# Layer 1 of a two-layer trunk: split weights kept in DRAM for the second half, the layer norm's channel adds on GpSimd with its mean products a step later

## The chip, the cores and the metric

The kernel runs on one core of a Trainium2 chip. The metric is the device time of one execution in microseconds (us). Each kernel is executed several times; the median counts, and one further execution is recorded by the hardware profiler, which gives the traces shown here. Line numbers (L1208) are those of the kernel before.

## The reference, cut to what matters

Layer 0 (attention and a gated MLP) is not touched. The change lies in layer 1, a causal convolution module over 2048 rows (tokens) of 1024 channels:

```python
def conv_layer(h, w_in, dw_w, dw_b, ln_g, ln_b, w_out):
    a, gl, z = jnp.split(h @ w_in, 3, axis=-1)        # h: (1, 2048, 1024), w_in: (1024, 3072)
    y = a * jax.nn.sigmoid(gl)
    y = lax.conv_general_dilated(y, dw_w[:, None, :], ...,  # depthwise, causal, 31 taps
                                 feature_group_count=CONV_WIDTH) + dw_b
    y = jax.nn.silu(layer_norm(y, ln_g, ln_b))        # norm over the 1024 channels
    return (y * jax.nn.silu(z)) @ w_out
...
x = x + rms_norm(conv_layer(rms_norm(x, g_pre), ...), g_post)
```

All of it is float32.

## The kernel before, in words

A float32 product is made of three: each operand is split into a rounded high part and a low part (`split`: a cast on ScalarE, ACT, and a subtraction, L125, on GpSimd, POOL, or VectorE, DVE), and high x high, high x low and low x high are summed in PSUM. 

Layer 1 (`tail`, from about 1520 us on) handles the rows in two halves of 1024. For each half, `layer1_in` runs 12 blocks, eight gated inputs ("g": a and gl for 128 channels) and four z gates ("z": 256 channels); the strings in `GATED` give their order in half 0 and half 1. Each block has one weight of 1024 x 256, four groups of 24 matmuls on TensorE (PE), and a `yield` behind each group, called a step here. `weights` keeps one weight ahead: at the start of a block the next one is loaded from the input into the one buffer `wraw`, and split into `whi` and `wlo`, of which there are two pairs, A and B, used in turn. All 12 weights are loaded and split in each half, so twice in all.

A gated input goes to a buffer `y` (six of them, also used as scratch by the norm) and into a queue of convolutions. A convolution is 31 taps on 128 channels x 1024 rows. DVE does a tap by one multiply-add into PSUM (`acc`, L1135); POOL does one by an add (L1102) of a product from ACT (L1101). A planner shares the taps out as the program is written: `beat` moves a clock on by 5.12 us a step, and emits taps for an engine while the engine's own clock, kept by `busy` with written costs (a POOL add 2.4, a weight split 4.5, a DVE tap 1.2 or 1.33), is behind. `drain` emits all that is left of some convolutions. Results go to DRAM (`yc_d`), as the z gates do (`z_d`). All DMAs are issued by SyncE (SP), in order.

The layer norm works on chunks of 256 rows with channels on the partitions (`gated_norm`, a generator of eight steps): load eight channel blocks from `yc_d`; add the blocks up (L1215 for 1024 columns, `fold` L1203 and L1204 for 512 and 256) and let PE sum over the partitions with a matrix of 1/1024 (`mean`, L1208); subtract, square (ACT), add (L1225, POOL); fold again, a second product for the variance; square root and reciprocal; load z and scale (L1246); silu on ACT and the product with z on POOL (L1254); split for the next product. The adds of L1215, L1203 and L1204 are on DVE, and the product is emitted in the same step as they are. In `tail`, `l(c, m)` runs chunk c's norm up to step m. Chunks 0 to 2 have most of their steps inside half 1; chunks 3 to 7 run one per output chunk.

The output projection (`out2`) takes a chunk as two tiles of 128 rows with two groups of 24 matmuls each; DVE and POOL then do the rms norm, the residual add (L875) and SP the store. Its weight comes in four pieces (`wout_pieces`), each loaded raw (pieces 0, 1 and 2 through `wraw`, piece 3 through `h6`), cast on ACT and subtracted on DVE, while half 1 ends.

The program is laid out by a scheduler when it is built: it places instructions on their engines roughly in the order written, but lets one pass another that is not ready in its own reckoning. On the chip each engine runs its list in order.

Of the kernel before, what the change touches and what calls it, by code (L numbers as in the profile page):

```python
# [19 lines left out]
P = 128  # L20
# [24 lines left out]
GATED = "ggggzggzggzz", "gggggzggzgzz"  # L45
# [36 lines left out]
class Trunk:  # L82
# [151 lines left out]
    def setup(self):  # L234
# [15 lines left out]
        self.z_d = dr.tile([D, S], F32, name="z_d", tag="z_d")  # L250
        self.taps = self.tile(c, [P, KT, TAPS], F32, "taps")
# [554 lines left out]
    def wout_pieces(self, W, raws, places, which, w, lo):  # L806

        nc = self.nc
        w = w if w else {}
        for i in which:  # L810
            n, h = divmod(i, 2)
            w[n, h] = [self.tile(pool, [P, 4, 512], F32R, *tag) for pool, *tag in places[i]]
            pool, tag, *bufs = raws[i]
            raw = self.tile(pool, [P, 4, 512], F32, tag, *bufs)
            nc.sync.dma_start(raw, W[512 * h:512 * h + 512, 512 * n:512 * n + 512]
                              .rearrange("(k p) n -> p k n", p=P))
            self.split(*w[n, h], raw, nc.scalar, lo)
        return w
# [139 lines left out]
    def layer1_in(self, inner, half, hs):  # L958
# [5 lines left out]
        def load():  # L964
# [3 lines left out]
            kind, k = self.plan[i]  # L968
            if kind == "g":
# [9 lines left out]
            where, tag = ((pool, "A"), (inner, "B"))[i % 2]  # L979
            hi = self.tile(where, [P, KT, 256], F32R, "whi" + tag)  # L980
            lo = self.tile(where, [P, KT, 256], F32R, "wlo" + tag)
            self.split(hi, lo, raw, nc.scalar, nc.gpsimd)
            self.busy("p", 4.5)
# [192 lines left out]
    def gated_norm(self, c, hand):  # L1176
# [25 lines left out]
        def fold(s):  # L1202
            v.tensor_tensor(s[:, 0:2], s[:, 0:2], s[:, 2:4], ALU.add)  # L1203
            v.tensor_tensor(s[:, 0], s[:, 0], s[:, 1], ALU.add)  # L1204
# [10 lines left out]
        v.tensor_tensor(s, Y[0], Y[1], ALU.add)  # L1215
        fold(s)
        m = mean(s)
        self.busy("v", 2.1)
        yield
# [9 lines left out]
        fold(sq[0])  # L1229
        var = mean(sq[0])  # L1230
        self.busy("v", 0.9)
        yield
# [38 lines left out]
    def tail(self, w1):  # L1271

        with ExitStack() as ctx:
# [44 lines left out]
            for i in range(1, 44):  # L1318
                step(z)
                for c in range(3):  # L1320
                    l(c, min(7, i + 1 - c))
# [3 lines left out]
            wout = lambda which, w=None: self.wout_pieces(self.a["odd_w_out"][0], [(lp, "wraw")] * 3 + [(lp, "h6")], places, which, w, self.nc.vector)  # L1325
# [6 lines left out]
            w = wout([2, 3], w)  # L1332
            for c in range(n):
# [9 lines left out]
                step((t0, t0)[c == 0]), self.beat(5.12 if c == 0 else 0)  # L1343
# [68 lines left out]
```

## Time and profile before

| | us |
|---|---|
| runs (three) | 2270.82 to 2274.74 |
| median | 2273.02 |
| the profiled execution | 2272.01 |
| its span (first to last instruction) | 2270.3 |

| engine | busy us | share of the span |
|---|---|---|
| PE (matmul) | 2201.3 | 97% |
| DVE | 1548.2 | 68% |
| ACT | 1258.6 | 55% |
| POOL | 1400.1 | 62% |

The mean granted clock of PE over the span is 0.993 of the full one. In the views below, a wait "PE A L1208 <- DVE y L1204" says that PE stood idle before an instruction of line 1208, and that what ended last before it could start was DVE's instruction of line 1204. A wait for several things is put down to the last of them, so a name can mislead where that engine had long been done. A group's "x16" is its number of instructions. A stretch "1860.00:1865.00" is in us from the start of the span.

### The profile page before, as it was taken

The numbers are of one execution on the slowest core, as the hardware profiler recorded it, in microseconds if no ns is written. First come the engines' busy times: TensorE is split into PE (matmuls) and PEld (weight loads), VectorE is DVE, ScalarE is ACT, GpSimd is POOL, SyncE is SP. The second block draws the span as 40 slices with busy tenths as digits, with TensorE's granted clock in tenths as the row PEclk, the third lists the DMA queues.
The fourth block names the chain that finished last, engine by engine and source line by source line (L and its number), as shares of the span: only waits on it lengthen the run. The fifth ranks groups of instructions, "written<-read, shape, count | busy, mean of one in ns | idle before, by whom it ended". The sixth has DMA issues, their size and how long they took to land.

```text
span 2270.3 us, 34584 instructions
## 1 busy us (share of the span) xinstructions
PE 2201.3 (97%) x12414; PEld 1905.8 (84%) x12414; DVE 1548.2 (68%) x3273; ACT 1258.6 (55%) x2345; POOL 1400.1 (62%) x1350
## 2 busy tenths in 40 slices
PE   8999999999989999999999999999999989998998
PEld 7898889988878999898998978888888778886877
DVE  3441324465248998888889954518998899999772
ACT  5231232253258888878888863435555475556463
POOL 5231222243237778667779644548998579999683
PEclk9999999999989999999999999999999999999999
DMA  6352231442281111100113154651222432224641
GB/s 157 98 195 84 79 107 53 148 136 85 89 234 52 35 41 29 29 20 27 29 55 109 44 176 152 225 174 47 84 85 81 140 104 65 75 93 151 220 167 65
DMA packets 244860, 229.19 MB, mean 101 GB/s; under 512 B 33841, under 2 KB 206897, under 8 KB 244432
## 3 DMA queue, kind: packets, MB, share of 16 engines
q1 hardware_dynamic: 244688, 226.98, 31.6%
q8 instruction: 98, 1.61, 0.3%
q14 instruction: 74, 0.61, 0.1%
HBM read 157.73 MB, written 69.21 MB: 100 GB/s over the span
## 4 chain that ended last, share of the span: by engine, by line
PE 64%; DVE 14%; POOL 10%; issue 5%; ACT 3%; DMA 2%; SPq 1%; DVEq 0%; POOLq 0%; ACTq 0%
POOL cacc L1102 8%; PE T L708 7%; PE A L161 7%; PE A L162 7%; PE A L163 7%; DVE acc L1135 6%; PE O L731 4%; PE A L576 4%; PE O L730 4%; PE A L577 4%; PE A L842 4%; PE A L843 4%; PE A L844 4%; PE A L173 2%; PE A L175 2%
## 5 line engine op out<-in xcount | busy, mean ns | idle before, releaser
L1135 DVE SCALAR_TENSOR_TENSOR acc<-y,const_taps,acc 128x1024 f32<-128x1024 f32 x304 | 378.9, 1282 | 4.0
L1102 POOL TENSOR_TENSOR cacc<-cacc,prod 128x1024 f32<-128x1024 f32 x145 | 371.7, 2570 | 14.6 <-ACT prod L1101 7.4
L125 POOL TENSOR_TENSOR wlo<-wraw,whi 128x2048 fp32r<-128x2048 f32 (+1 forms) x26 | 120.9, 4649 | 314.2 <-ACT whi L122 279.3
L125 DVE TENSOR_TENSOR ptl<-T,pth 128x512 fp32r<-128x512 f32 (+1 forms) x414 | 263.8, 659 | 20.8 <-ACT pth L122 18.0
L122 ACT CAST pth<-T 128x512 fp32r<-128x512 f32 (+1 forms) x414 | 221.9, 580 | 51.4 <-PE T L708 41.1
L1101 ACT ACTIVATE prod<-y,const_taps 128x1024 f32<-128x1024 f32 x145 | 165.2, 1149 | 140.8 <-POOL cacc L1102 140.6
L161 PE MATMUL A<-hhi,whi 128*128 128x512 f32 x608 | 237.8, 391 | 0.0
L163 PE MATMUL A<-hhi,wlo 128*128 128x512 f32 x608 | 236.7, 389 | 0.0
L162 PE MATMUL A<-hlo,whi 128*128 128x512 f32 x608 | 236.7, 389 | 0.0
L685 POOL TENSOR_SCALAR Ps<-Ps,attn_ssm,gates 128x256 f32<-128x256 f32 (+15 forms) x128 | 161.9, 1265 | 112.1 <-DVE attn_ssm L682 78.2
L730 PE MATMUL O<-pth,V 128*128 128x256 f32 x824 | 220.5, 292 | 0.0
L731 PE MATMUL O<-ptl,V 128*128 128x256 f32 x824 | 219.4, 293 | 1.1 <-POOL ptl L717 0.4
L576 PE MATMUL A<-K,q 128*128 128x320 f32 (+4 forms) x544 | 206.8, 384 | 9.1 <-DVE attn_smx L580 4.4
L577 PE MATMUL A<-K,q 128*128 128x320 f32 (+4 forms) x544 | 183.6, 343 | 0.0
L680 ACT ACTIVATE Ps<-Ps,attn_nm 128x256 f32<-128x256 f32 (+15 forms) x128 | 155.9, 1218 | 31.4 <-DVE attn_nm L678 29.3
L580 DVE CUSTOM_DVE_ANT_1 Ps<-A,attn_bm 128x512 f32<-128x512 f32 (+3 forms) x264 | 154.8, 611 | 22.8 <-PE A L577 11.4
L708 PE MATMUL T<-ident,Ps 128*128 128x128 f32 x1088 | 164.2, 273 | 2.2 <-DVE ptl L125 1.8
L731 PEld LDWEIGHTS O<-ptl,V 128*128 128x128 f32 x824 | 155.4, 189 | 8.6 <-DVE ptl L125 4.2
L730 PEld LDWEIGHTS O<-pth,V 128*128 128x128 f32 x824 | 155.6, 189 | 2.5
L161 PE MATMUL A<-h,whiB 128*128 128x512 f32 x384 | 149.7, 390 | 1.2 <-ACT b L1026 1.2
L162 PE MATMUL A<-h,whiA 128*128 128x512 f32 x384 | 150.8, 393 | 0.0
L161 PE MATMUL A<-h,whiA 128*128 128x512 f32 x384 | 149.8, 392 | 0.7 <-DVE y L1008 0.7
(388 smaller groups left out, 6198.1 us busy)
## 6 DMA issues: line engine op xcount, KB each, us to landing
wraw<-in_even_w_in_dram SPq DMA_DIRECT2D x24, 1024.0 KB, 6.0
q<-q_d SPq DMA_DIRECT2D x128, 128.0 KB, 2.8
wraw<-in_odd_w_in_dram SPq DMA_DIRECT2D x32, 512.0 KB, 4.6
x<-x_d SPq DMA_DIRECT2D x21, 512.0 KB, 3.4
a_d<-osum SPq DMA_DIRECT2D x128, 64.0 KB, 2.1
x<-in_x_dram SPq DMA_DIRECT2D x16, 512.0 KB, 5.5
x_d<-x SPq DMA_DIRECT2D x16, 512.0 KB, 2.9
wraw<-in_odd_w_in_dram SPq DMA_DIRECT2D x8, 1024.0 KB, 5.0
```

The costliest lines, as they stand in the source:

```text
L122: self.nc.scalar.copy(hi, src)
L125: lo_eng.tensor_tensor(lo, src, hi.bitcast(F32), ALU.subtract)
L161: nc.tensor.matmul(o, whi[:, k, wk], hhi[:, k], start=(k == 0), stop=False)
L162: nc.tensor.matmul(o, whi[:, k, wk], hlo[:, k], start=False, stop=False)
L163: nc.tensor.matmul(o, wlo[:, k, wk], hhi[:, k], start=False, stop=(k == KT - 1))
L576: nc.tensor.matmul(out, q[:, 0, r, :], K[:, g, ks], start=True, stop=False)
L577: nc.tensor.matmul(out, q[:, 1, r, :], K[:, g, ks], start=False, stop=True)
L708: nc.tensor.transpose(pt[:, c:c + P], ps[r], self.ident)
L730: nc.tensor.matmul(O, v, hi[:, c], start=(i + j == 0), stop=False)
L731: nc.tensor.matmul(O, v, lo[:, c], start=False, stop=(i + j == len(items) - 1))
L1102: nc.gpsimd.tensor_tensor(c["sum"], c["sum"], t, ALU.add)
L1135: v.scalar_tensor_tensor(acc, win, w, old, ALU.mult, ALU.add)
```

## The change

Half 0 stores every split weight (high and low part, 1 MB each) in a new DRAM buffer `w_d`, and half 1 loads both parts from there straight into `whi` and `wlo`; the planner counts no split for them. In half 1 the order of blocks has the last gated input two blocks earlier. In the layer norm the adds of the channel blocks go from DVE to POOL, with new written costs, and each mean product is emitted a step after its adds. The norms of chunks 0 to 2 start two steps later and lie three steps apart instead of one. Chunk 1's norm is finished ahead of the first output group, and one norm step in each output chunk lies earlier than before. Output weight pieces 1 and 3 are loaded and split in two parts each, through the small buffers `b4`; pieces 0 and 2 use `wraw`.

```diff
--- before.py
+++ after.py
@@ -42,7 +42,7 @@
 LEFT, RIGHT = 96, 224
 LATE = 2
 OUT1 = [5, 7, 6, 4, 1, 3, 2, 0, *range(8, NT)]
-GATED = "ggggzggzggzz", "gggggzggzgzz"
+GATED = "ggggzggzggzz", "ggggggzggzzz"
 LEAD = 5.12
 AHEAD = 8.0
 
@@ -248,6 +248,7 @@
         self.x1_d = dr.tile([S, D], F32, name="x1_d", tag="x1_d")
         self.yc_d = dr.tile([D, S], F32, name="yc_d", tag="yc_d")
         self.z_d = dr.tile([D, S], F32, name="z_d", tag="z_d")
+        self.w_d = dr.tile([12, 2, P, KT * 256], F32, name="w_d", tag="w_d")
         self.taps = self.tile(c, [P, KT, TAPS], F32, "taps")
         self.cb = self.tile(c, [P, KT], F32, "cb")
         self.ident = self.tile(c, [P, P], F32, "ident")
@@ -811,10 +812,12 @@
             n, h = divmod(i, 2)
             w[n, h] = [self.tile(pool, [P, 4, 512], F32R, *tag) for pool, *tag in places[i]]
             pool, tag, *bufs = raws[i]
-            raw = self.tile(pool, [P, 4, 512], F32, tag, *bufs)
-            nc.sync.dma_start(raw, W[512 * h:512 * h + 512, 512 * n:512 * n + 512]
-                              .rearrange("(k p) n -> p k n", p=P))
-            self.split(*w[n, h], raw, nc.scalar, lo)
+            r = 2 if bufs else 4
+            for k in range(0, 4, r):
+                raw = self.tile(pool, [P, r, 512], F32, tag, *bufs)
+                nc.sync.dma_start(raw, W[512 * h + P * k:512 * h + P * (k + r), 512 * n:512 * n + 512]
+                                  .rearrange("(k p) n -> p k n", p=P))
+                self.split(*(t[:, k:k + r] for t in w[n, h]), raw, nc.scalar, lo)
         return w
 
     def wout_early(self):
@@ -966,6 +969,16 @@
             if i == 24:
                 return
             kind, k = self.plan[i]
+            where, tag = ((pool, "A"), (inner, "B"))[i % 2]
+            hi = self.tile(where, [P, KT, 256], F32R, "whi" + tag)
+            lo = self.tile(where, [P, KT, 256], F32R, "wlo" + tag)
+            flat = lambda t: t.rearrange("p k n -> p (k n)").bitcast(F32)
+            kept = self.w_d[k + 8 * (kind == "z")]
+            if i >= 12:
+                for t, d in zip((hi, lo), kept):
+                    nc.sync.dma_start(flat(t), d)
+                self.ws.append((hi, lo))
+                return
             if kind == "g":
                 pieces = [W[:, n * D + P * k:n * D + P * k + P] for n in range(2)]
             else:
@@ -976,10 +989,9 @@
                 w = p.shape[1]
                 nc.sync.dma_start(raw[:, :, o:o + w], p.rearrange("(k p) n -> p k n", p=P))
                 o += w
-            where, tag = ((pool, "A"), (inner, "B"))[i % 2]
-            hi = self.tile(where, [P, KT, 256], F32R, "whi" + tag)
-            lo = self.tile(where, [P, KT, 256], F32R, "wlo" + tag)
             self.split(hi, lo, raw, nc.scalar, nc.gpsimd)
+            for t, d in zip((hi, lo), kept):
+                nc.sync.dma_start(d, flat(t))
             self.busy("p", 4.5)
             self.ws.append((hi, lo))
 
@@ -1200,8 +1212,8 @@
                               .rearrange("(i c) t -> c i t", c=P))
 
         def fold(s):
-            v.tensor_tensor(s[:, 0:2], s[:, 0:2], s[:, 2:4], ALU.add)
-            v.tensor_tensor(s[:, 0], s[:, 0], s[:, 1], ALU.add)
+            nc.gpsimd.tensor_tensor(s[:, 0:2], s[:, 0:2], s[:, 2:4], ALU.add)
+            nc.gpsimd.tensor_tensor(s[:, 0], s[:, 0], s[:, 1], ALU.add)
 
         def mean(s):
             o = self.tile(*self.pt)
@@ -1212,11 +1224,11 @@
             load(Y[q], self.yc_d, q)
         yield
         s = tmp()
-        v.tensor_tensor(s, Y[0], Y[1], ALU.add)
+        nc.gpsimd.tensor_tensor(s, Y[0], Y[1], ALU.add)
         fold(s)
+        self.busy("p", 4.4)
+        yield
         m = mean(s)
-        self.busy("v", 2.1)
-        yield
         sq = []
         for y in Y:
             v.tensor_tensor(y, y, wide(m), ALU.subtract)
@@ -1227,9 +1239,9 @@
         self.busy("p", 2.3)
         yield
         fold(sq[0])
+        self.busy("p", 2.0)
+        yield
         var = mean(sq[0])
-        self.busy("v", 0.9)
-        yield
         rs = self.tile(self.late_conv, [P, 256], F32, "lrs", 1)
         nc.scalar.activation(rs, var, AF.Sqrt, bias=self.eps)
         v.reciprocal(rs, rs)
@@ -1318,11 +1330,11 @@
             for i in range(1, 44):
                 step(z)
                 for c in range(3):
-                    l(c, min(7, i + 1 - c))
+                    l(c, min(7, i - 1 - 3 * c))
             step(z)
             places = [[(lp, "whiA"), (lp, "wloA")], [(lp, "h0"), (lp, "h1")],
                       [(inner, "whiB"), (inner, "wloB")], [(lp, "h4"), (lp, "h5")]]
-            wout = lambda which, w=None: self.wout_pieces(self.a["odd_w_out"][0], [(lp, "wraw")] * 3 + [(lp, "h6")], places, which, w, self.nc.vector)
+            wout = lambda which, w=None: self.wout_pieces(self.a["odd_w_out"][0], [(lp, "wraw"), (lp, "b4", 5)] * 2, places, which, w, self.nc.vector)
             w = wout([0])
             step(z, 2)
             w = wout([1], w)
@@ -1330,6 +1342,7 @@
             l(0, 8)
             step(z, 3)
             w = wout([2, 3], w)
+            l(1, 8)
             for c in range(n):
                 t0, t1 = (self.out2(c, i, hand[c], w, gpost) for i in range(2))
                 if c == 2:
@@ -1340,7 +1353,9 @@
                 l(c + 1, 8), l(c + 2, 2)
                 step((t0, t1)[c == 0]), self.beat()
                 l(c + 2, 3)
-                step((t0, t0)[c == 0]), self.beat(5.12 if c == 0 else 0)
+                step(t0)
+                l(c + 2, 4)
+                self.beat(5.12 if c == 0 else 0)
                 step((t1, t0)[c == 0]), self.beat(5.12 if c else 0)
                 l(c + 2, 5)
                 step(t1), self.beat()
```

## Rows read from the trace of the kernel before

**Rows 1.** The page, part 1: engine, busy us (share of the span), instructions.

```profile
PE 2201.3 (97%) x12414; PEld 1905.8 (84%) x12414; DVE 1548.2 (68%) x3273; ACT 1258.6 (55%) x2345; POOL 1400.1 (62%) x1350
```

**Rows 2.** PE's waits, 1500 to 2271 us: who, for whom; total us, times, longest.

```profile
PE A L1208 <- DVE late_ors L866: 5.3, 2, 4.1
PE T L1208 <- DVE y L1204: 4.3, 1, 4.3
PE A L842 <- ACT late_ors L865: 3.3, 1, 3.3
PE A L843 <- DVE h L125: 2.7, 1, 2.7
PE A L843 <- DVE wloB L125: 2.1, 1, 2.1
PE T L1208 <- DVE Y L1222: 1.8, 1, 1.8
```

**Rows 3.** Stretches: PE, PEld, DVE, ACT, POOL busy us; granted clock, DMA share, GB/s.

```profile
1860.00:1865.00 5.00, 4.82 (x15) 3.97 (x16) 5.00 (x6) 2.61 (x5) 0.45 (x1) 0.68 0.01 2
...
2080.00:2085.00 5.00, 4.41 (x13) 3.46 (x13) 5.00 (x4) 3.32 (x4) 4.92 (x2) 0.67 0.62 210
...
2095.00:2100.00 5.00, 3.74 (x9) 3.00 (x10) 4.96 (x8) 1.09 (x4) 5.00 (x3) 0.53 0.48 137
...
2100.00:2105.00 5.00, 5.00 (x19) 4.00 (x18) 3.13 (x3) 0.24 (x1) 5.00 (x3) 0.79 0.79 283
...
2190.00:2195.00 5.00, 4.56 (x13) 3.67 (x14) 4.86 (x7) 1.76 (x2) 2.38 (x2) 0.66 0.51 184
```

**Rows 4.** The norm's lines one by one: duration ns min/median/max, first and last start, shapes.

```profile
L1215 DVE TENSOR_TENSOR y<-x,x x2: 1216/1220/1225, 1804.0 to 1811.2; 128x1024 f32<-128x1024 f32 x2
...
L1203 DVE TENSOR_TENSOR y<-y x6: 676/1732/4504, 1805.8 to 1850.7; 128x512 f32<-128x512 f32 x6
...
L1204 DVE TENSOR_TENSOR b<-b x10: 424/2488/2618, 2092.7 to 2212.7; 128x256 f32<-128x256 f32 x10
...
L1225 POOL TENSOR_TENSOR b<-b,b x5: 2394/2412/2852, 2116.4 to 2209.4; 128x1024 f32<-128x1024 f32 x5
```

**Rows 5.** Stretches as above, of L1215, then L1203, then L1204 alone: DVE busy us.

```profile
1780.00:2271.00 491.00, 17.38 (x8) 0.98 0.35 120
...
1780.00:2271.00 491.00, 24.73 (x16) 0.98 0.35 120
...
1780.00:2271.00 491.00, 28.64 (x16) 0.98 0.35 120
```

**Rows 6.** Groups by form, POOL and DVE: shapes, count | busy us, mean ns | idle before.

```profile
L1102 POOL TENSOR_TENSOR cacc<-cacc,prod 128x1024 f32<-128x1024 f32 x145 | 371.7, 2570 | 14.6 <-ACT prod L1101 7.4
...
L125 POOL TENSOR_TENSOR wloA<-wraw,whiA 128x2048 fp32r<-128x2048 f32 x12 | 56.5, 4710 | 19.9 <-ACT whiA L122 19.8
...
L615 POOL TENSOR_TENSOR attn_pad<-attn_pad,ctmp 128x128 f32<-128x128 f32 x72 | 33.2, 461 | 2.2
...
L927 POOL TENSOR_TENSOR wloA<-wloA 128x512 f32<-128x512 f32 x5 | 6.5, 1302 | 2.2 <-DMA wloA<-a_d 2.2
...
L1135 DVE SCALAR_TENSOR_TENSOR acc<-y,const_taps,acc 128x1024 f32<-128x1024 f32 x160 | 197.7, 1280 | 1.3
```

**Rows 7.** DMA issues, 1500 to 2271 us: out<-in, count, KB each, us to landing.

```profile
wraw<-in_odd_w_in_dram SPq DMA_DIRECT2D x8, 1024.0 KB, 5.0
```

**Rows 8.** The DMA queue's own waits (SP), same stretch, columns as in PE's waits.

```profile
SPq L1144 <- DVE cout L1135: 40.4, 5, 18.9
```

**Rows 9.** PE in order of time: start us, us, line, instruction; two group starts, a mean product.

```profile
1741.17 0.39 PE L161 MATMUL A<-h,whiA 128*128 128x512 f32 x1
...
1746.61 0.39 PE L161 MATMUL A<-h,whiA 128*128 128x512 f32 x1
...
2112.27 0.59 PE L1208 MATMUL T<-b,mean 128*128 128x256 f32 x2
```

**Rows 10.** Stretch of the tail, all engines, columns as in the other stretches.

```profile
2120.00:2240.00 120.00, 114.51 (x496) 93.66 (x495) 86.62 (x85) 68.89 (x123) 88.36 (x34) 0.99 0.41 146
```

## The prediction

> **What bounds the kernel now.** I read the page's busy shares first: TensorE (PE) is busy 97% of the span [rows 1]. With PE that full, a change that leaves PE's work alone can only return the time in which PE stands still, or runs at its lower clock. So the second view is PE's own waits, taken from 1500 us on, where layer 1 runs [rows 2]. They come in three places. (a) The layer norm of the first chunks inside half 1, at 1841 to 1860 us: 4.3 us before a mean product (L1208) whose adds on DVE (L1204) were late and 1.8 us before another; with 0.7 us for an eviction beside them that makes 6.7 us idle. (b) The change-over to the output projection, 2063 to 2096 us: 2.7, 2.1 and 0.7 us for pieces of the split output weights, 3.3 us for a PSUM bank that a lagging DVE had not yet emptied, 0.2 us for the first normed chunk: 9.0 us. (c) The tail, to 2195 us: 5.3 us before mean products (put down to L866, a short reciprocal that DVE ran right behind an L1204), 0.2 us beside, 5.5 us. (Four of these waits are of 0.7 us or less; their rows are left out.)
>
> The third view is the granted clock in slices of 5 us [rows 3]. Behind each of the three places the mean falls between the two levels, 1.2 and 2.4 GHz: to 0.68 of the upper one behind (a), 0.67, 0.53 and 0.79 behind (b), 0.66 behind (c). Busy PE time times the share not granted is what that costs: 4.82 x 0.32 = 1.5 us for (a); 4.41 x 0.33 + 3.74 x 0.47 + 5.0 x 0.21 = 4.3 us for (b); 4.56 x 0.34 = 1.6 us for (c). So the most that this change can return is 8.2 + 13.3 + 7.1 = 28.6 us.
>
> The fourth view says why DVE was late. One of the norm's 256-column adds on DVE takes 0.42 us at best, 2.49 us in the median; a 512-column add 0.68 to 4.5 us; a 1024-column add can take 1.22 us [rows 4]. All three have both inputs in SBUF, and what the long ones have in excess is about one POOL add of 1024 columns, 2.41 us [rows 4]. The conv taps, with the sum in PSUM, keep a mean of 1.28 us [rows 6]. The 40 adds on these three lines together hold DVE 17.4 + 24.7 + 28.6 = 70.7 us [rows 5]; at their short durations they would take 8 x 1.22 + 16 x 0.68 + 16 x 0.42 = 27.4 us. Some 43 us of DVE time is waiting for POOL.
>
> **The change, part by part.** *Weights.* Twelve weights of half 1 are no longer split. That takes 12 POOL subtractions of 4.7 us, 56 us, and as many ACT casts off [rows 6]. The planner is code with written costs (L1102's add is 2.4, a split 4.5): replaying its sums gives 145 POOL taps for the kernel before, which is what the trace has [rows 6], and 153 after, with 319 DVE taps for 325. In its plan the last convolution is through some 10 us sooner, at planned 487 instead of 497. In half 0 each split weight is also stored: 24 stores of 1 MB. SP's next raw load already waits for the same POOL subtraction as the store of the low part, so no wait on the queue is new there. A raw load behind two stores lands up to 2 x 5.0 us later [rows 7], with 21.8 us of PE work a block to hide in (four groups of 24 products, 5.44 us each [rows 9]). I take nothing; without that cover it would be 2 or 3 us a block.
>
> In half 1 two loads of 1 MB take the place of one, and they wait on SP for PE to leave the slot, one block ahead of use. At 5.0 us for 1 MB [rows 7] they need 5 us side by side to 10 us in a row, beside 21.8 us. Behind them on SP stand stores of finished convolutions, stores of the z gate and the norm's loads; whoever waits for those is up to a block later, and none is due sooner than that. I take 0. Ahead of them on SP may stand a convolution's store, for which SP has waited as long as 18.9 us [rows 8]: that is a rival below.
>
> *Norm adds on POOL.* DVE loses 70.7 us. POOL gets per chunk one add of 1024 columns (2.41 us in the median [rows 4]; taps average 2.57), two of 512 (1.30 us) and two of 256, which has no row; it lies between 0.46 us for 128 columns and 1.30 us for 512 [rows 6], nearest to the first, and I take 0.74. Together 2.41 + 1.30 + 0.74 = 4.45 us before the mean and 2.04 us before the variance, 6.5 us a chunk, 52 us for eight. So POOL loses 56, gains 52, and gets eight more taps, 21 us; it is about as busy as before, but in other places. The Trainium skill (GPSIMD Engine Reference, section "Engine selection") speaks against this edit: it sends two-input adds to VectorE, about twice as fast. Undisturbed the rows agree (1.22 to 2.41 us [rows 4]), but as they lie now, DVE's 40 adds hold it 70.7 us. By the page's ratio POOL would need about 2 x 27.4 = 55 us (an estimate), and the sum would be 3 us of POOL time worse.
>
> *Mean products a step behind.* PE's mean product was emitted with the adds it needs. Now a step of PE work, 5.44 us, lies between, against 4.45 and 2.04 us of adds. In half 1 the norms of chunks 0, 1 and 2 also start three steps apart instead of one. In the replay POOL's clock is past PE's at four of six products there, by 0.2, 3.6, 2.9 and 1.4 us; the plan counts 5.12 us a step where PE takes 5.44, which gives some of that back. So new waits in half 1 are between 0 and 8.1 + 4 x 1.5 (clock) = 14 us. I take 2.5 us, near the low end, because of that slack of 0.3 us a step. POOL's queue behind those adds holds taps, which have no due time within a step.
>
> *Order of the gates, output weights.* The last gated input of half 1 comes four steps earlier, so taps don't pile up at the end. Output weight pieces 1 and 3 land in four small buffers instead of the one that piece 0 and 2 use, so piece 2's load no longer waits for piece 1's split; chunk 1's split is emitted ahead of the first output group. DVE then has no norm adds and three instead of eight taps left (replay), so the 9.0 us of (b) lose their causes one by one. What may stay is chunk 0's own split on POOL, two adds of 2.4 us after PE frees their slot: 0.2 us as now, to 6 us with the clock. I take 1.5 us.
>
> *Tail.* Per chunk of 256 rows PE has 96 x 0.2267 + 2 x 0.59 = 22.9 us of work [rows 9]. POOL had seven adds of 1024 columns, 16.9 us; now 16.9 + 6.5 = 23.4 us. It is as long as PE's. POOL had 120 - 88.4 = 31.6 us free in 2120 to 2240 us [rows 10], and the norms run up to two chunks ahead, so I expect the work to fit with little to spare. New or remaining waits are from 0 to 14 us (twice what is there now); I take 4 us.
>
> **The sum.** 28.6 us returned, less 2.5 + 1.5 + 4 = 8.0 us new: 20.6 us. The profiled execution took 2272.0 us (span 2270.3), so 2251.4; the median of the runs is 1.0 us above the profiled one, so I predict 2252.5 us. All low ends give 2244.5; all high ends at once (14 + 6 + 14) would give 2278.5.
>
> **The rivals.** *Slower: POOL bounds the norms.* If POOL's free time in the tail is not spare but waiting that the chain of steps imposes (for ACT's silu, say), it stays: 31.6 us over 5.2 chunks is 6.1 us a chunk, and a chunk takes 23.4 + 6.1 = 29.5 us, 6.6 more than PE. Five chunks, 33 us, with (a) and (b) still won (21.5 us): 2284 us. It decides against the change once more than 4.3 us a chunk stay. (The rule of GPSIMD Engine Reference in the Trainium skill points to this case.) Against it: waits for DVE's adds go, and POOL's own adds are up to 0.4 us longer beside them (2.41 to 2.85 us [rows 4]). Chance 0.10. *Slower: weights late.* If SP stands behind a convolution's store as long as it once did, a load lands 18.9 + 10 us after the slot is free, 7.1 us late; with seven convolutions ending in half 1 that is 50 us, 2302 us. It needs a load later than 11.8 us after the slot; before, SP reached such stores early, not late. Chance 0.03. *Partly.* The order on each engine is settled when the program is built, so the mean product can still stand right behind its adds, or POOL run late by one add per product: (b) is won, (a) and (c) turn from a wait for DVE into one for POOL: 2262 to 2268. Chance 0.16. *No difference.* The gaps were slack that PE loses elsewhere, for example at chunk 0's split and at the evictions: 2268 to 2277. Chance 0.09.
>
> **How the numbers follow.** My forecast has 0.62, with a range of its own from 2243 to 2262. Faster by over 0.2% (below 2268.5; 0.2% is about what a measurement of this kernel can tell from no change) is 0.62 + 0.16 = 0.78; within 0.2% 0.09; slower 0.10 + 0.03 = 0.13. The range for 8 in 10 goes from 2243 to 2272, into the case of no difference.
>
> **What would show it.** Right: no wait of PE before L1208's successor over 2 us in half 1, no wait for split output weights, a granted clock at 1.0 from 1860 to 2200 us, DVE under 50% in the tail, POOL near full in it. 153 POOL taps and 12 large POOL subtractions in layer 1 show the plan. Wrong: PE waiting for POOL adds at most mean products, or at the start of half 1's blocks for a load of stored weights.

## The result, and the profile after

The changed kernel takes 2294.05 us in the median (four runs, 2287.64 to 2295.0; before, four runs, 2271.92). Its ratio to the kernel before is 1.0084 [1.0073, 1.0096]: slower by 0.84%, where I had forecast 0.9% faster. Its profiled execution took 2293.22 us with a span of 2291.5 us. Line numbers from here on are those of the changed kernel: the norm's adds are L1227 (1024 columns), L1215 and L1216 (512 and 256), the mean products L1220, the splits L125, the output matmuls L845 to L847.

The page, part 1, after (columns as in [rows 1]):

```profile
PE 2208.8 (96%) x12414; PEld 1909.7 (83%) x12414; DVE 1480.9 (65%) x3228; ACT 1245.7 (54%) x2341; POOL 1405.6 (61%) x1386
```

DVE lost 67 us of work, POOL's sum hardly moved: the two shifts that I had counted. PE's busy time grew by 7.5 us at the same number of instructions; its clock was lower for longer (granted 0.986 over the span, before 0.993). PE's waits after, 1500 to 2292 us (who, for whom; total us, times, longest):

```profile
PE A L847 <- POOL h L125: 9.5, 5, 3.9
PE A L845 <- DVE yn L877: 8.6, 3, 4.3
PE A L845 <- ACT h L122: 5.6, 2, 3.3
PE A L846 <- DVE wloB L125: 4.7, 1, 4.7
PE A L845 <- ACT b L1038: 3.6, 1, 3.6
PE acc L212 <- DVE cout L1153: 2.0, 1, 2.0
```

Beside [rows 2], no wait before a mean product is left. New in the tail is the wait for `h`, a chunk's own cast and split (L122, L125), the last step of its norm. Stretches of before, then of after (PE, PEld, DVE, ACT, POOL busy us; granted clock, DMA share, GB/s):

```profile
1760.00:1785.00 25.00, 21.11 (x102) 16.55 (x101) 24.79 (x24) 15.74 (x19) 24.61 (x10) 1.00 0.30 106
1820.00:2040.00 220.00, 213.27 (x932) 175.63 (x931) 218.74 (x166) 130.61 (x145) 207.09 (x74) 0.99 0.25 82
2040.00:2100.00 60.00, 51.00 (x205) 40.20 (x205) 58.85 (x48) 37.23 (x43) 58.53 (x21) 0.93 0.42 143
2100.00:2180.00 80.00, 78.74 (x343) 64.56 (x341) 65.41 (x61) 43.06 (x76) 57.73 (x23) 0.99 0.59 209
```

```profile
1760.00:1785.00 25.00, 20.42 (x91) 16.45 (x90) 23.61 (x23) 15.63 (x19) 23.73 (x10) 0.86 0.44 162
1820.00:2040.00 220.00, 219.51 (x968) 181.12 (x967) 213.31 (x167) 129.60 (x149) 203.73 (x88) 1.00 0.36 134
2040.00:2100.00 60.00, 49.18 (x202) 39.20 (x201) 49.17 (x39) 30.23 (x38) 53.93 (x21) 0.91 0.63 219
2100.00:2180.00 80.00, 67.70 (x281) 53.61 (x280) 24.94 (x36) 33.81 (x62) 56.29 (x31) 0.93 0.35 127
```

Half 1 (1820 to 2040) went as hoped: PE 219.5 of 220 us at full clock. The tail did not: 281 matmul records in 2100 to 2180 instead of 343, and a clock of 0.93.

**A ledger.** Three marks on PE's timeline cut the span: the last matmul of half 1's input norm (L212), the first and the last output matmul. Before they lie at 1813.9, 2062.5 and 2263.8 us, after at 1816.8, 2057.9 and 2285.1; behind the last mark both need 6.5 us. The stretch between the output marks, "the tail" from here on, is 201.3 us before and 227.2 after. 768 matmuls of 0.2267 us and 10 mean products of 0.59 us make 180.0 us, the rest is loss. I divide it in two. Loss A, the change-over, is 60 us less PE's busy time times its clock in 2040 to 2100 us: before 60 - 51.00 x 0.93 = 12.6, after 60 - 49.18 x 0.91 = 15.2. (It takes in the last 18 us of half 1, where little is lost; in other kernels the first output matmul lies at 2055 to 2069 us.) Loss B is what remains of the tail: before 201.3 - 180.0 - 12.6 = 8.7, after 32.0. So the 21.2 us of span are: +3.0 before half 1, -7.6 in half 1, +2.6 A, +23.3 B.

**Where B comes from.** The timeline of chunk 4's norm after its variance product (start us, us, engine, line, instruction; in brackets the idle time ahead of it and what ended it):

```profile
2158.44 0.59 PE L1220 MATMUL A<-b,mean 128*128 128x256 f32 x2
2159.07 0.47 ACT L1246 ACTIVATE lrs<-A,l_eps 128x256 f32<-128x256 f32 x1 [1.10 <-PE A L1220]
2159.58 1.75 DVE L1247 RECIPROCAL lrs<-lrs 128x256 f32<-128x256 f32 x1 [1.43 <-ACT lrs L1246]
2161.25 2.29 DVE L1234 TENSOR_TENSOR Y<-Y,A 128x1024 f32<-128x1024 f32 x2
2163.52 2.34 DVE L1258 TENSOR_TENSOR Y<-Y,lrs 128x1024 f32<-128x1024 f32 x2
2165.95 2.08 ACT L1264 ACTIVATE Y<-Y,l_cv 128x256 f32<-128x256 f32 x4
...
2169.35 2.36 POOL L1266 TENSOR_TENSOR Y<-Y,Z 128x1024 f32<-128x1024 f32 x1
2171.68 2.33 POOL L878 TENSOR_TENSOR x<-x,yn 128x1024 f32<-128x1024 f32 x1
...
2173.96 0.50 PE L845 MATMUL A<-whiA,h 128*128 128x512 f32 x1 [3.32 <-ACT h L122]
2173.99 1.28 POOL L1215 TENSOR_TENSOR b<-b 128x512 f32<-128x512 f32 x1
2175.23 2.35 POOL L1266 TENSOR_TENSOR Y<-Y,Z 128x1024 f32<-128x1024 f32 x1
2177.55 0.72 POOL L1216 TENSOR_TENSOR b<-b 128x256 f32<-128x256 f32 x1
2178.23 2.33 POOL L125 TENSOR_TENSOR h<-Y,h 128x1024 fp32r<-128x1024 f32 x1
2180.62 0.79 PE L847 MATMUL A<-whiA,h 128*128 128x512 f32 x1 [3.88 <-POOL h L125]
```

From the variance product to the first split's end are 22.1 us. It is a chain of dependent instructions over ACT, DVE, ACT, POOL, ACT, POOL, and between its links stand pieces of the next chunk's norm (L1234, L1215, L1216) and the last chunk's residual add (L878). PE's list of instructions gives it less: after the variance product of chunk 4 come 49 matmuls and one mean product, 49 x 0.2267 + 0.6 = 11.7 us, and then the first matmul that needs the chunk. PE waits 3.32 and 3.88 us, and the matmul behind the second wait takes 0.79 us, at the lower clock (granted 0.50 from 2180 to 2185 us). I call the number of matmuls between the two the lead.

Over all five chunks of the tail (3 to 7) these chains take 23.4, 22.1, 23.2, 14.9 and 17.1 us in the trace, and their leads, at 0.2267 us a matmul, are worth 13.8, 11.1, 15.4, 15.6 and 8.4 us. Only chunk 6's chain fits its lead, and chunk 6 is the only one of the five that PE does not wait for. Before, chains of 14.3 to 21.2 us had leads of 18.4 to 27.2 us, and each fitted. The 8.6 us put down to `yn` are waits for a PSUM bank that DVE's eviction (L877) has to empty. The two long ones, 3.8 and 4.3 us, fall after PE has begun chunks 3 and 5 with the high parts alone; the first splits of these chunks end at 2147.7 and 2210.7 us, at most 0.3 us ahead of the matmul that takes them, so an earlier bank would have returned next to nothing. From 2100 us on PE stands idle for 21.2 us; behind these waits the clock is lower (granted 0.92 from there to the last output matmul), and that makes up the rest of B.

### The profile page after: what moved, and what is told of

Same layout as the page of the kernel before. It is cut to its first block, busy times and chain, and to the rows that moved or that the text cites. A ratio compares the mean times of both kernels' runs of the same rounds, so it can differ in the third digit from the quotient of the medians.

```text
span 2291.5 us, 34632 instructions
## 1 busy us (share of the span) xinstructions
PE 2208.8 (96%) x12414; PEld 1909.7 (83%) x12414; DVE 1480.9 (65%) x3228; ACT 1245.7 (54%) x2341; POOL 1405.6 (61%) x1386
## 4 chain that ended last, share of the span: by engine, by line
PE 68%; POOL 12%; DVE 10%; issue 5%; ACT 3%; DMA 1%; SPq 1%; DVEq 0%; POOLq 0%; ACTq 0%
POOL cacc L1114 8%; PE T L709 7%; PE A L161 7%; PE A L162 7%; PE A L163 7%; DVE acc L1147 5%; PE O L732 4%; PE A L847 4%; PE A L577 4%; PE A L845 4%; PE A L846 4%; PE O L731 4%; PE A L578 4%; PE A L175 2%; PE A L177 2%
## 5 line engine op out<-in xcount | busy, mean ns | idle before, releaser
L1114 POOL TENSOR_TENSOR cacc<-cacc,prod 128x1024 f32<-128x1024 f32 x153 | 387.7, 2539 | 22.5 <-ACT prod L1113 9.5
L1147 DVE SCALAR_TENSOR_TENSOR acc<-y,const_taps,acc 128x1024 f32<-128x1024 f32 x297 | 372.5, 1282 | 4.7
L125 POOL TENSOR_TENSOR wlo<-wraw,whi 128x2048 fp32r<-128x2048 f32 (+1 forms) x26 | 120.9, 4649 | 313.9 <-ACT whi L122 278.8
L125 DVE TENSOR_TENSOR ptl<-T,pth 128x512 fp32r<-128x512 f32 (+1 forms) x414 | 263.9, 660 | 20.8 <-ACT pth L122 18.0
L122 ACT CAST pth<-T 128x512 fp32r<-128x512 f32 (+1 forms) x414 | 221.9, 580 | 50.6 <-PE T L709 41.0
L1113 ACT ACTIVATE prod<-y,const_taps 128x1024 f32<-128x1024 f32 x153 | 174.6, 1150 | 130.8 <-POOL cacc L1114 130.5
L161 PE MATMUL A<-h,whiB 128*128 128x512 f32 x384 | 151.0, 393 | 1.4 <-ACT b L1038 1.4
L162 PE MATMUL A<-h,whiB 128*128 128x512 f32 x384 | 150.8, 393 | 0.0
L163 PE MATMUL A<-h,wloB 128*128 128x512 f32 x384 | 150.6, 392 | 0.0
```

The costliest lines, as they stand in the source:

```text
L122: self.nc.scalar.copy(hi, src)
L125: lo_eng.tensor_tensor(lo, src, hi.bitcast(F32), ALU.subtract)
L161: nc.tensor.matmul(o, whi[:, k, wk], hhi[:, k], start=(k == 0), stop=False)
L162: nc.tensor.matmul(o, whi[:, k, wk], hlo[:, k], start=False, stop=False)
L163: nc.tensor.matmul(o, wlo[:, k, wk], hhi[:, k], start=False, stop=(k == KT - 1))
L1114: nc.gpsimd.tensor_tensor(c["sum"], c["sum"], t, ALU.add)
```

## The experiments

The results with the ledger. Chips differ, so a kernel is placed by its ratio to the kernel before on its own chip; "won" is 1.0084 less that ratio, times 2272 us. The last columns are read from each program's list for PE, chunks 3 to 7: matmuls from mean to variance product, and the lead from variance product to chunk. The columns tail, A and B come from the one profiled execution of each kernel, which lies between 4 us below the median (e4) and 7 us above it (e12).

| kernel | median us | ratio [95%] | won us | tail | A | B | mean to var | lead |
|---|---|---|---|---|---|---|---|---|
| before | 2271.92 | 1 | | 201.3 | 12.6 | 8.7 | 53-74 | 81-120 |
| after | 2294.05 | 1.0084 [1.0073, 1.0096] | 0 | 227.2 | 15.2 | 32.0 | 72-103 | 37-69 |
| e6 | 2289.67 | 1.0074 [1.0059, 1.0089] | 2 | 222.4 | 10.3 | 32.1 | 72-103 | 37-69 |
| e8 | 2294.52 | 1.0090 [1.0073, 1.0106] | -1 | 227.2 | 15.2 | 32.0 | 72-103 | 37-69 |
| e4 | 2277.40 | 1.0018 [1.0008, 1.0027] | 15 | 210.7 | 13.3 | 17.4 | 67-98 | 46-92 |
| e7 | 2271.26 | 0.9994 [0.9981, 1.0006] | 20 | 205.1 | 13.3 | 11.8 | 57-108 | 68-107 |
| e3t | 2269.70 | 0.9986 [0.9977, 0.9995] | 22 | 206.6 | 14.6 | 12.0 | 57-108 | 68-107 |
| e3 | 2264.94 | 0.9960 [0.9945, 0.9975] | 28 | 199.6 | 6.9 | 12.7 | 57-108 | 68-107 |
| e5b | 2273.47 | 0.9997 [0.9988, 1.0006] | 20 | 198.1 | 7.8 | 10.3 | 55-80 | 88-120 |
| e9 | 2269.38 | 0.9978 [0.9970, 0.9987] | 24 | 205.0 | 15.2 | 9.8 | 55-80 | 88-120 |
| e1 | 2268.13 | 0.9976 [0.9965, 0.9987] | 25 | 200.0 | 14.5 | 5.5 | 54-67 | 77-90 |
| e2 | 2263.28 | 0.9945 [0.9925, 0.9964] | 32 | 198.9 | 15.1 | 3.8 | 54-67 | 77-90 |
| e11 | 2259.74 | 0.9935 [0.9923, 0.9948] | 34 | 192.9 | 9.2 | 3.7 | 54-67 | 77-90 |
| e12 | 2256.83 | 0.9932 [0.9918, 0.9945] | 35 | 193.6 | 8.8 | 4.8 | 54-67 | 77-90 |

Kernels with the same order in the tail have the same B, within 2 us, whatever A is. The first theories were three: the norm's chain stands in POOL's list too often (A in the expectations); the products a step behind come too late (B); the output weights or the weight loads are late (C). Later ones were POOL's load as such (A') and the lead (D). These letters have nothing to do with the losses A and B of the table.

**e1, e2: the adds back on DVE**, in all chunks (e1) or chunks 3 to 7 (e2), the products still a step behind.

```diff
-            nc.gpsimd.tensor_tensor(s[:, 0:2], s[:, 0:2], s[:, 2:4], ALU.add)
+            e.tensor_tensor(s[:, 0:2], s[:, 0:2], s[:, 2:4], ALU.add)
...
+        e, adds = (nc.gpsimd, (("p", 4.4), ("p", 2.0))) if c < 3 else (v, (("v", 2.1), ("v", 0.9)))
```

> The changed kernel with the channel adds of all eight chunks back on DVE; products still a step behind, stored weights kept. Theory A: tail as with the adds of chunks 3 to 7 on DVE, and half 1 loses what the adds on POOL gave it there (up to 8 us): 2272 to 2282. Theory B: 2290 to 2300, chain over 75 us. Theory C: 2285 to 2300.

> The changed kernel, with the channel adds of chunks 3 to 7 (the tail) back on DVE; products still a step behind. In the changed kernel a chunk's norm takes 76 to 83 us from its first add to its last split (chunks 4 to 7; before 54 to 59), and PE waits 33 us in the tail and the change-over. Theory A (the norm's chain now goes through POOL's queue five times instead of three, each time behind other chunks' work): the chain falls back to 60 us or less and the time by 15 to 25 us, to 2270 to 2279. Theory B (the mean products a step behind lengthen the chain, whichever engine adds): the chain stays at 75 us or more and the time within 5 us of 2294. Theory C (the new order of output weights and of chunk 1's split holds the tail up): time within 8 us of 2294.

Measured: 0.9976 and 0.9945, loss B down to 5.5 and 3.8. Both come out 4 to 7 us below the range of theory A, the nearest. The adds on POOL in the tail are needed for the loss; leaving those of half 1 on POOL gains a little (e2 against e1: 7 us by the ratios, 2 us by the profiled spans).

**e3, e3t: each product in the step of its adds**, in all chunks (e3) or chunks 3 to 7 (e3t), the adds still on POOL.

```diff
-        self.busy("p", 4.4)
-        yield
         m = mean(s)
+        self.busy("p", 4.4)
+        yield
```

> The changed kernel with each mean product again in the same step as its adds; the adds stay on POOL. Theory A: the chain stays near 80 us and the time at 2288 to 2300. Theory B: the chain shortens by about two steps of 5.4 us for each of two products and the time falls to 2270 to 2280. Theory C: 2288 to 2300.

> The changed kernel with the mean products of chunks 3 to 7 alone emitted in the step of their adds; chunks 0 to 2, in half 1, keep them a step behind. Adds stay on POOL. The theory of the lead (POOL's adds and a step behind, together, leave the rest of the norm too few matmuls in the tail) puts the whole effect of the step behind into chunks 3 to 7: this kernel should come out as the one with all products in the step of their adds, 2262 to 2268 us, with some 200 us from the first output matmul to the last. The rival, that what is gained by products right behind their adds comes from half 1 (its products stand earlier, and more taps follow), gives 2285 to 2295 us with a tail of 220 us or more.

Measured: 0.9960 and 0.9986; loss B is 12.7 and 12.0. e3 is 5 us below the range of theory B, the nearest. So the step behind is needed for the loss as well. With e2 this speaks against POOL alone and against the step alone: undoing either returns 19 us of B or more. The expectation of e3t was missed by 1.7 us (2269.70 in the median against at most 2268): the tail's order does return B, but e3 has 7.7 us less A, and all that differs is where the products of half 1 stand (more at e12).

**e7: the norm's steps in the tail emitted one step earlier**, the engines and all else as after.

```diff
-                l(c + 1, 8), l(c + 2, 2)
+                l(c + 1, 8), l(c + 2, 3)
...
-                l(c + 2, 3)
+                l(c + 2, 4)
```

(and so for the steps 4, 5, 7 and the first of chunk c + 3)

> The changed kernel, adds on POOL and products a step behind as they are; only in the tail each norm step of chunks 3 to 7 is emitted one step earlier. Theory D (lead): what costs the time is how few matmuls stand on PE between a chunk's variance product and the first output matmul that needs the chunk, in the changed kernel 61, 49, 68, 69 and 37 for chunks 3 to 7 (8 to 16 us), where the rest of the norm (root, scaling, silu, gate, split) takes 22 to 28 us. One step earlier gives 71, 92, 85, 68 and 107, the same order of PE as with the products in the step of their adds: the time falls to 2260 to 2270. Theory A' (POOL's load as such, 23.4 us a chunk, is too much): the same adds on the same engine, so the time stays within 8 us of 2294.

Measured: 0.9994, loss B 11.8. At 2271.26 us it lies 1.3 us above the range of the lead's theory, and 15 us below that of POOL's load. This run decides: no add changed its engine, every product is still emitted a step behind its adds; the lead grew, from 37-69 to 68-107, to the same order of PE as in e3t, and with it came the same B. The chains themselves are no shorter, 18 to 26 us. What stays of B goes with that: chunk 3, with a chain of 22.4 us against a lead of 16.3 us, still keeps PE waiting 3.3 us for its split. The stretch 2100 to 2260 us of after, then of e7:

```profile
2100.00:2260.00 160.00, 140.03 (x575) 111.68 (x574) 54.19 (x73) 73.21 (x134) 111.04 (x58) 0.93 0.34 120
```

```profile
2100.00:2260.00 160.00, 150.69 (x646) 122.64 (x645) 66.88 (x78) 76.54 (x140) 126.07 (x61) 0.98 0.34 124
```

POOL is busy 126 of 160 us in the quicker kernel and 111 in the slower one. POOL's capacity did not bound the changed kernel; 49 of its 160 us were idle in it.

**e4: POOL relieved.** The residual add of the output goes to DVE in the tail, a fifth of POOL's work there.

```diff
-            nc.gpsimd.tensor_tensor(x, x, t, ALU.add)
+            (nc.gpsimd if banks else nc.vector).tensor_tensor(x, x, t, ALU.add)
```

> The changed kernel with the residual add of the output tiles of layer 1 (L875 of before, two of 2.4 us a chunk) on DVE. POOL's load in the tail falls by a fifth, from 23.4 to 18.6 us a chunk; PE has 72, 46, 67, 67 and 92 matmuls between variance product and first use. Theory A' (load of POOL): 2262 to 2275. Theory D (lead): the lead stays short but for chunk 7, so most of the loss stays: 2277 to 2292.

Measured: 1.0018, loss B 17.4. It is just inside the lead's range and 2 us above that of POOL's load. The edit returns 15 us, less than the longer lead of e7 does. How much of it is one POOL instruction less between the links of the chain is not shown, since the order changed with it and the lead grew too (46-92).

**e9: both**, the adds of chunks 3 to 7 on DVE and the steps one earlier.

> The changed kernel with the adds of chunks 3 to 7 on DVE and, on top of it, the norm's steps in the tail one step earlier. By the list of PE, 88 to 120 matmuls then stand between a variance product and its chunk, where 77 to 90 stand with the adds on DVE alone. The theory of the lead: once the lead is longer than the rest of the norm (15 to 21 us there, 66 to 93 matmuls), more lead is worth little: 2258 to 2265 us, against 2263. Rival: the earlier norm takes the engines from the output projection's own eviction and residual add, as its steps do with the adds on POOL in the same place (2271): 2266 to 2273 us.

Measured: 0.9978, the rival's value: 8 us behind e2. Loss B rose from 3.8 to 9.8. PE's waits in e9 and e2:

```profile
PE A L1222 <- DVE late_ors L869: 5.4, 2, 2.9
...
PE A L1222 <- DVE late_oss L860: 1.9, 1, 1.9
```

```profile
PE A L1222 <- DVE late_ors L869: 3.2, 2, 2.5
```

With the lead at 88-120, what is late is the other end: from 2100 us on PE waits before mean or variance products (L1222 here) alone, 7.6 us in all (one wait of 0.3 us is left out), against 3.2 in e2. More lead than the chain needs was no gain here.

**e6, e11: the output weights and chunk 1's norm as before the change**, with the adds on POOL (e6) or on DVE in chunks 3 to 7 (e11).

```diff
-            wout = lambda which, w=None: self.wout_pieces(..., [(lp, "wraw"), (lp, "b4", 5)] * 2, ...)
+            wout = lambda which, w=None: self.wout_pieces(..., [(lp, "wraw")] * 3 + [(lp, "h6")], ...)
...
-            l(1, 8)
```

> The changed kernel with the output weights' pieces loaded as before (three through one buffer, one through another) and without the earlier end of chunk 1's norm. PE's order in the tail is the same as in the changed kernel. Theory D: tail as long (225 us or more from the first output matmul to the last), time 2286 to 2300; the change-over gets no better. If the new order of output weights were the cause (theory C): under 2280.

> The changed kernel with the adds of chunks 3 to 7 on DVE and the output weights loaded and split as before the change, chunk 1's norm not finished ahead of the first output group. With the adds on POOL this part was worth 4.4 us. If the change-over is a place of its own (waits of 4.6 and 3.6 us and a granted clock of 0.91 from 2040 to 2100 us with the adds on DVE), it is worth about as much here: 2257 to 2261 us. If its waits only stand ahead of the tail's norm and come back there, 2262 to 2266 us.

Measured: 1.0074, so the output weights are not the cause; and 0.9935, in the first range. For e6 the time came in the range expected, but the change-over got better and the tail is 222.4 us, not 225 or more. Loss A is 4.9 us lower in e6 than in the changed kernel and 5.9 us lower in e11 than in e2: in these traces the new way of the output weights, together with the earlier end of chunk 1's norm, made the change-over worse, not better. The times alone don't show it: the intervals of e6 and the changed kernel overlap, and so do those of e11 and e2. The stretch 2040 to 2100 us of e2, then of e11:

```profile
2040.00:2100.00 60.00, 49.32 (x203) 39.18 (x202) 52.42 (x43) 30.76 (x39) 49.57 (x18) 0.91 0.61 206
```

```profile
2040.00:2100.00 60.00, 54.00 (x222) 42.64 (x220) 47.89 (x40) 30.52 (x37) 48.19 (x18) 0.94 0.58 205
```

**e12: e11 with half 1's products in the step of their adds.**

> The kernel of the run before (adds of chunks 3 to 7 on DVE with their products a step behind, output weights as before the change), with the mean products of chunks 0 to 2 now in the step of their adds on POOL; the order of PE's matmuls from the first output matmul on is unchanged. With the adds on POOL everywhere, products in the same step in half 1 gave 232 matmul records from 2040 to 2100 us at a clock of 0.97, products a step behind 204 at 0.89, and 7 us less from the first output matmul to the last. If the step behind in half 1 makes the change-over late (chunk 1's last norm steps then fall on ACT and DVE together with the last pieces of the output weights), this kernel has a clock over 0.96 from 2040 to 2100 us and takes 2253 to 2257 us. If that gain hung on the output weights in four small pieces, which this kernel does not have, it takes 2258 to 2262 us.

Measured: 0.9932, within e11's interval; loss A 8.8 against 9.2, clock 0.94. The median, 2256.83 us, falls in the first range, but the kernel before was 3.2 us quicker on this chip than on e11's; by the ratio and by the clock the second reading holds: where the output weights come as before, no difference in A shows wherever half 1's products stand. Of the kernels with stored weights, A is high (13.3 to 15.2) where the new output weight pieces meet products a step behind in half 1, and 6.9 to 10.3 where at least one of the two is missing (e3, e5b, e6, e11, e12). By what path the products act on it, I did not find.

**e5b: the kernel before, with the stored weights and the new order of the gates alone.**

```diff
-GATED = "ggggzggzggzz", "gggggzggzgzz"
+GATED = "ggggzggzggzz", "ggggggzggzzz"
...
+            if i >= 12:
+                for t, d in zip((hi, lo), kept):
+                    nc.sync.dma_start(flat(t), d)
```

> The kernel before with two parts of the change alone: split weights kept in DRAM, and the last gated input two blocks earlier. Norm adds on DVE, products and output weights as before. Theories A and B both put the loss in the norm: this kernel is 3 to 12 us faster than the kernel before (2260 to 2269), because POOL is rid of 56 us of subtractions in half 1. Should the loads or stores of the weights hold PE up, PE waits at the starts of blocks in half 1 and the time is 2275 or more.

Measured: 0.9997, no difference, so the gain of 3 to 12 us did not come, and the 2275 us of late weights did not either. (By the strings of `GATED` the last gated input comes one block, four steps, earlier, not two.) Its tail is 3.2 us shorter, its half 1 starts 5.7 us later and the first output matmul 6.5; half 1 itself is as long as before (249.4 us against 248.7). No load was late: in none of the traces with stored weights does PE wait for one.

**e8: a written cost of 4.5 us for half 1's first weight**, as if it were still split, to test whether the changed share of taps slows the start of half 1.

```diff
+                if i == 12:
+                    self.busy("p", 4.5)
```

> The changed kernel with one line more: the planner counts 4.5 us on POOL for the thirteenth weight (the first that is loaded and not split), as it did before, so that the taps of half 0 are shared out as before. Between 1760 and 1785 us the changed kernel lost some 4 us to a wait of PE for a convolution's last add on DVE and a lower clock (0.86) behind it. If that comes from the changed plan: 2288 to 2292 and a clock of 1.0 there; if from the stores and loads of the weights: no change, 2294.

Measured: 1.0090, no difference to the changed kernel; the clock of 0.86 in 1760 to 1785 us stayed.

## Why the prediction was wrong

**What bounds the kernel, and half 1: right in the outcome.** Place (a) was won; no wait before L1220 in half 1, and 219.5 of 220 us at full clock. Half 1 became 7.6 us shorter, where 8.2 - 2.5 = 5.7 were forecast. That the adds had to leave DVE for this is not borne out: with the adds back on DVE in all chunks (e1) half 1 takes 241.6 us, the changed kernel 241.0, before 248.7. The stretch 1820 to 2040 us of e1:

```profile
1820.00:2040.00 220.00, 217.55 (x959) 179.52 (x958) 202.62 (x162) 129.66 (x149) 195.86 (x79) 1.00 0.36 135
```

Stored weights and gates alone (e5b) do not bring it, and e3, without the step behind, has it too (240.7 us). What all the kernels with a short half 1 share beyond e5b is the new starts and spacing of the norms; no run tests these alone.

**The plan, the weights: right in the counts, too good in the sum.** 153 POOL taps stand in the trace (387.7 us, 2539 ns each). The 12 large POOL subtractions are there too. No load was late; a low part took 8.0 to 8.1 us to land in the median, within the 5 to 10 us that I had reckoned with. But at the start of half 1 something is lost that I had not looked for. PE's stretches of before and of after there:

```profile
1770.00:1775.00 5.00, 4.61 (x22) 3.39 (x20) 4.93 (x5) 2.03 (x3) 5.00 (x3) 1.00 0.67 199
1775.00:1780.00 5.00, 2.56 (x15) 1.75 (x15) 4.96 (x6) 3.66 (x6) 4.84 (x3) 1.00 0.29 115
```

```profile
1770.00:1775.00 5.00, 1.99 (x7) 1.56 (x8) 4.93 (x5) 3.84 (x6) 4.84 (x3) 0.75 0.26 107
1775.00:1780.00 5.00, 5.00 (x14) 3.88 (x14) 4.96 (x7) 3.19 (x4) 4.84 (x3) 0.57 0.00 0
```

Idle time there was before, too, but in pieces, and the clock stayed up. After, a wait of 2.0 us (0.4 before) for a convolution's last add (`cout`) lengthens it, and the clock falls: 1.99 x 0.25 + 5.0 x 0.43 = 2.6 us. All kernels with stored weights show it, e5b too. Why that add now ends later against PE is open; e8 only excludes the planner's cost of one weight.

**Change-over, place (b): wrong.** I took 1.5 us of remaining loss, on the reasoning that the 9.0 us of waits "lose their causes one by one". A is 15.2. In the timeline after, taps of half 1's end stand ahead of the weights:

```profile
2063.90 8.36 POOL L1114 TENSOR_TENSOR cacc<-cacc,prod 128x1024 f32<-128x1024 f32 x3
2067.32 1.16 ACT L1113 ACTIVATE prod<-y,const_taps 128x1024 f32<-128x1024 f32 x1 [5.59 <-POOL cacc L1114]
2068.38 1.98 ACT L122 CAST h<-x 128x1024 fp32r<-128x1024 f32 x2
2070.26 1.99 ACT L122 CAST h<-b 128x1024 fp32r<-128x1024 f32 x2
2073.21 1.88 ACT L122 CAST whiB<-wraw 128x2048 fp32r<-128x2048 f32 x1
2075.64 0.50 PE L845 MATMUL A<-whiB,h 128*128 128x512 f32 x1 [3.63 <-ACT b L1038]
2077.76 3.24 DVE L125 TENSOR_TENSOR wloB<-wraw,whiB 128x2048 fp32r<-128x2048 f32 x1
2081.05 0.80 PE L846 MATMUL A<-wloB,h 128*128 128x512 f32 x1 [4.68 <-DVE wloB L125]
```

ACT's list has a product for a POOL tap in front; ACT waits 5.59 us for POOL to free its buffer, then casts chunk 1 and weight piece 3, and only then piece 2 (`whiB`, `wloB`), which PE needs first. (PE's wait of 3.63 us is put down to L1038, a neighbour of that cast that ended last.) Each cause that I had seen was a resource; what came in its place, as this timeline reads, is order on ACT. No run tests that by itself. The forecast of no wait for output weights was wrong (3.6 and 4.7 us); chunk 0's own split, the one loss that I had allowed for, took 2.5 us, within its 0.2 to 6.

**Tail, place (c): wrong, and the term that decides.** I took 4 us, bounds 0 to 14; B went from 8.7 to 32.0. The step that failed is "the norms run up to two chunks ahead, so I expect the work to fit". It set POOL's work a chunk (23.4 us) against PE's (22.9): a sum of busy times. What counts is a chain's length against its lead. Two edits, each of little harm alone (B 3.8 to 5.5 with the step behind only, 12.7 with the adds on POOL only, 8.7 before), act on the lead from both ends. With the adds on POOL the variance product stands further back in PE's list, 72-103 matmuls behind the mean product instead of 53-74 before and 54-67 in e1 and e2; the step behind moves both products back (mean product to chunk 140-160 matmuls instead of 134-190). 37 to 69 matmuls, 8 to 16 us, were left for chains of 15 to 23 us. I priced the move of the products in half 1 alone; in the tail, where it had its effect, I gave it no term.

**The rivals.** "POOL bounds the norms" (chance 0.10, 2284 us) has the sign and nearly the size: B rose by 23.3 us over five chunks, 4.7 us a chunk, just over the 4.3 that I gave as its turning point. Its condition, POOL time that "the chain of steps imposes", is what the trace shows (49 of 160 us idle, beside a chain that is late); its name is wrong, since e3 and e7 leave all adds on POOL and return 19 and 20 us of B. It expected (a) and (b) won; (b) was not, which is the rest. "Weights late" did not happen. Of the signs that I listed, DVE under 50% in the tail came true (24.9 of 80 us); a clock of 1.0 to 2200 us did not; PE did not wait for POOL adds, and POOL was not near full (56.3 of 80 us): the sign for "wrong" was sought at the mean products, while PE waited one chain later.

**The choice of engine.** The Trainium skill (GPSIMD Engine Reference, section "Engine selection") sends two-input adds to VectorE. In the tail its advice held: e2 is 32 us faster than the changed kernel. Its reason, POOL about twice as slow, fits the shortest adds alone (424 to 716 ns at 256 columns), not the medians. The adds of 1024 columns and of 256, on DVE in e2 and on POOL in after (duration ns min/median/max):

```profile
L1229 DVE TENSOR_TENSOR b<-Y x4: 1583/2964/3139, 2110.6 to 2183.7; 128x1024 f32<-128x1024 f32 x4
L1218 DVE TENSOR_TENSOR b<-b x10: 424/1462/2506, 2090.9 to 2215.0; 128x256 f32<-128x256 f32 x10
```

```profile
L1227 POOL TENSOR_TENSOR b<-Y x4: 2405/2408/2422, 2105.7 to 2191.5; 128x1024 f32<-128x1024 f32 x4
L1216 POOL TENSOR_TENSOR b<-b x10: 716/738/772, 2091.7 to 2241.7; 128x256 f32<-128x256 f32 x10
```

In the tail, with POOL at work beside them, the DVE adds are the longer ones, in the median 2.96 to 2.41 us and 1.46 to 0.74. The Trainium skill's page SBUF — State Buffer (section "SBUF: two separate sides") describes an exclusive lock between the two engines. These rows and [rows 4] agree with it: the longest DVE add of 256 columns takes 2.1 us more than the shortest, less than one POOL add of 1024 columns (2.41 us). e2 is faster although its adds take longer: POOL's list is left to the end of the chain, which then takes 14.3 to 16.8 us, and the variance product stands earlier in PE's list, so that each chain fits its lead of 17.5 to 20.4 us.

**A faster kernel.** e11 and e12 beat both: 0.9935 [0.9923, 0.9948] and 0.9932 [0.9918, 0.9945], with stored weights, half 1's adds on POOL, the tail's on DVE, and the output weights as they were. The two cannot be told apart, nor, by the intervals, from e2.

## What to carry to other kernels

Where engines run lists in a fixed order, cost a moved step by its lead: count the work that stands between it and the first user of its result, and set that against the whole chain behind it, with what other engines have queued between its links; busy sums only say that it could fit. A step moved later and a step made longer act on the same lead, so such edits are priced together, in every place where the moved code runs. And when a wait is to go away, follow the chain on from there to the first instruction that needs its end, and look for waits there too.

## What the runs showed that I had not expected

The durations of the adds on POOL hardly spread. Their medians in the tail are what I had taken (0.74 us for 256 columns, 1.29 for 512, 2.41 for 1024), and of the 25 that write the buffers `b` all but one are within 0.06 us of these; that one, of 512 columns, took 2.28 us. In e2 the adds of 256 columns on DVE vary by a factor of six (424 to 2506 ns).

And of the clock, two stretches with idle time in them, from the start of half 1. Before, PE was busy 3.94, 4.61 and 2.56 of 5 us in three slices in a row, and the granted clock stayed at 1.00, the upper level. After, it was busy 3.43 and 1.99 of 5 us, and the granted clock was 0.75 in the second slice and 0.57 in the one behind it, which PE filled. The first slices of the two, before and after:

```profile
1765.00:1770.00 5.00, 3.94 (x24) 3.16 (x23) 4.93 (x5) 3.39 (x5) 5.00 (x2) 1.00 0.26 105
```

```profile
1765.00:1770.00 5.00, 3.43 (x21) 2.59 (x19) 4.96 (x5) 2.99 (x4) 4.92 (x3) 1.00 0.70 289
```
